# Seven products for both column halves of an FFN's last block pair, with weight sums made by adding transfers

## The chip, the cores and the metric

The kernel runs on one core of one Trainium2 chip, in one launch. The metric is the device time of that core in microseconds (us). Three timed runs before the change gave 2164.31, 2165.05 and 2165.15 us, median 2165.05. The profile was taken from a further execution, which took 2164.99 us; its span, from the first to the last instruction, is 2163.2 us, so 1.8 us lie around it.

## The reference

Two layers work on 256 tokens of width 2048 in float32. Each layer has a mixer stage and then a dense SwiGLU FFN of hidden width 5632. Only the FFN matters here:

```python
h = rms_norm(x, g[2])
f = (jax.nn.silu(h @ ffn_w_gate[layer]) * (h @ ffn_w_up[layer])) @ ffn_w_down[layer]
x = x + rms_norm(f, g[3])
```

## The kernel before

**Three matmuls for one product.** A float32 weight tile of 128x1024 (512 KB) is split into a high part `whi`, a rounded copy (ScalarE, L198), and a low part `wlo`, the rest (VectorE, L200). Activations are split the same way. TensorE then computes high x high, high x low and low x high (L237 to L239, or L771 to L773 in the products below) into one PSUM bank. `halves` makes both parts; each pool of parts has 7 tiles. A weight chunk of 512x512 is two such tiles, and with 256 tokens and three matmuls for one product it costs 24 matmuls of 512 columns.

**Two streams of weights.** `wstream` is loaded by `load_half` (tile `raw`, 5 buffers) in the order of use. `sstream` holds the down-projection chunks for the block pairs and is loaded by `sload` (tiles `sw`), as two tiles for one chunk. Both are issued on SyncE's queue.

**The FFN.** The 5632 hidden columns are 11 blocks of 512: five pairs (`PAIRS`) and one lone block (`LONE` = 10). For each block `gate_up` computes gate, up and their product, transposed. For a pair of blocks, the token halves t = 0, 1, the blocks and two neighbouring output columns n0, n1 form a 2x2 by 2x2 block matrix product. `quads` computes it with seven products of 12 matmuls each, where the plain way has eight. `combos` makes the seven operand combinations of the activations (tiles `so`), and `form` makes the weight sums in place with VectorE additions of 128x1024 (L720), two for each sum (one for each tile of a chunk). The products are called b11, t1, t2, b22, t3, b21, t4. Each goes into a PSUM bank `sq` and is added from there to one or two accumulators `f`, or to a helper accumulator `fu` that is folded in at the end (L780; the fold is L644 and L646). The 2048 output columns are four pieces of 512, n = 0 to 3; a column half p holds pieces 2p and 2p+1.

**What runs beside what.** `quads` is a generator. The matmul loops call `tick`, which moves it on by `rate` steps for each unit of work; one step is one half product of 6 matmuls. The products of a pair so run spread over the `gate_up` of the next pair. Only those of the last pair run beside the lone block.

**The last pair before.** By `COLS`, the pair (8, 9) runs `quads` for p = 1 only, at rate .75 beside the lone block's gate and up, and what is left beside its down products. The left columns, n = 0 and 1, are computed plainly for blocks 8, 9 and 10 in `post` (three chunks of 24 matmuls for each n), where `operand` chooses b11, a21, b21, t4 or the lone block's `ht`. For n = 2 and 3 only block 10 is left. `before(2)` lets all products finish before n = 2 begins.

**After the last product.** `post` adds each `acc` bank to `f` (L508, VectorE), takes its sum of squares (L398, ScalarE), and multiplies by the gain `gb` (L561). For n = 0 (both t) and for n = 1 (t = 0) that multiplication runs on GpSimd; the others are on VectorE. GpSimd's instructions and the transfers that it issues (`gb` at L492, the reload of `x` at L790) stand in one queue.

Each engine takes its instructions in the order that the scheduler fixed when the kernel was built, and waits at the first one that isn't ready.

Of the kernel before, what the change touches and what calls it, by code (L numbers as in the profile page):

```python
# [18 lines left out]
F32 = mybir.dt.float32  # L19
# [16 lines left out]
PAIRS = [(0, 1), (2, 3), (4, 5), (6, 7), (8, 9)]  # L36
COLS = [(0, 1)] * 4 + [(1,)]
LONE = 10
# [6 lines left out]
RATE1, WIDTH1 = .9, 7  # L45
NCHUNK = 306
NQUAD = 72
LHALF = (9, 10, 331, 332)
AHEAD, SETTLE = 2, 4
ENDRATE = .75  # L50
LAG = 2
# [43 lines left out]
class Trunk:  # L95
    def __init__(self, tc, dr, out, stage=99):
        self.tc, self.nc, self.dr, self.out, self.stage = tc, tc.nc, dr, out, stage
        self.plan = []
        self.pending = deque()
        self.bg = []  # L100
        self.early = deque()
        self.script, self.later = None, deque()
        self.lag = 2 * LAG
        self.nraw = 0
        self.rate, self.width, self.credit = 1.0, 3, 0.0
        self.n = 0
# [4 lines left out]
        self.splan, self.sraw, self.squeue = [], {}, deque()  # L111

# [475 lines left out]
    def ffn(self, li, norm, after):  # L588
# [20 lines left out]
        self.rate, self.width = 1.0, 1  # L609
        for pi, pair in enumerate(PAIRS):  # L610
            self.squeue.extend((li, b, n) for p in COLS[pi] for b, n in (
                (pair[0], 2 * p), (pair[0], 2 * p + 1), (pair[1], 2 * p + 1), (pair[1], 2 * p)))
        for pi, pair in enumerate(PAIRS):
# [12 lines left out]
            while self.bg:  # L626
                self.step()
            ops = self.combos(h, pi == len(PAIRS) - 1)
            self.spawn(self.quads(li, pair, COLS[pi], ops, f, pi == 0))
        ht = self.new_xt(1, "ht")  # L630
# [4 lines left out]
        def before(n):  # L635

            if n == 2:
                while self.bg:
                    self.step()
                self.tight = False  # L640
# [7 lines left out]
        def operand(kt, t):  # L648
            b, k = kt // 4, kt % 4
            if b == 2:  # L650
                return self.xk(ht)(k, t)
            o = ops[(("b11", "a21"), ("b21", "t4"))[b][t]]
            return o[0][:, k], o[1][:, k]
        self.rate = ENDRATE
        gate_up(LONE, whole)
        seg = self.post(li, 3, 1, after, f[:2], before)
        own = [(b, 4 * i) for i, b in enumerate((*PAIRS[-1], LONE))]
        seg(lambda n: [("ffn_w_down", li, 512 * b, 512 * n, k) for b, k in (own[2:] if n > 1 else own)], operand)

    def sload(self):  # L660

        if not self.squeue:
            return
        li, b, n = self.squeue.popleft()
        with self.tc.high_priority():
            tiles = [self.slot([P, 1024], nm="sw") for _ in range(2)]
            for i, r in enumerate(tiles):
                self.tc.keep_in_program_order(self.nc.sync.dma_start(
                    out=r, in_=self.dr["sstream"][len(self.splan)][:, i * 1024:(i + 1) * 1024]))
        self.splan.append(("A", "ffn_w_down", li, 512 * b, 512 * n))  # L670
        self.sraw[li, b, n] = tiles

    def combos(self, h, whole):


        nc = self.nc
        out = {}

        def put(key, src):
            o = self.slot([P, 2, 4, P], F32R, "so")  # L680
            out[key] = o[:, 0], o[:, 1]
            part(key, src)

        def part(key, src):
            hi, lo = out[key]
            nc.scalar.copy(hi, src)
            nc.vector.tensor_sub(lo, src, hi.bitcast(F32))
        put("b11", h[0, 0])
# [13 lines left out]
        put("t3", k)  # L702
        if whole:
            out["a21"] = self.mtmp([P, 4, P], F32R, "a21"), self.mtmp([P, 4, P], F32R, "a21")
            part("a21", h[1, 0])
        return out

    def quads(self, li, pair, cols, ops, f, first):

        nc = self.nc  # L710
        for _ in range(SETTLE):
            yield
        for p in cols:
            n0, n1 = 2 * p, 2 * p + 1
# [47 lines left out]
            for key in order:  # L762
# [13 lines left out]
                for d, sign, new in into[key]:  # L776
                    if first and new:
                        nc.scalar.copy(d, ps)
                    else:
                        (nc.vector.tensor_add if sign > 0 else nc.vector.tensor_sub)(d, d, ps)  # L780
                yield

# [834 lines left out]
```

## Time and profile before

| what | value |
|---|---|
| median of three runs | 2165.05 us |
| profiled execution | 2164.99 us, span 2163.2 us |
| TensorE busy | 2146.1 us, 99% |
| VectorE busy | 1741.8 us, 81% |
| ScalarE busy | 1244.1 us, 58% |
| GpSimd busy | 133.8 us, 6% |
| moved by DMA | 428.72 MB |

In profile rows PE is TensorE, PEld its weight loads, DVE VectorE, ACT ScalarE, POOL GpSimd and SP SyncE; a q behind the name is that engine's sequencer. A row of a group of instructions gives line, engine, operation, output tile, input tile, shape and count, then the busy time in us and the mean duration of one in ns, then the idle time ahead of them and what ended it. A row of the timeline gives the start in us, the duration in us, and the instruction; neighbours of one kind are merged, with their count. A matmul of 512 columns is recorded with 0.39 us but the next one starts after about 0.23 us, since matmuls are pipelined.

### The profile page before, as it was taken

To read this page: it belongs to the slowest core of one execution; us is meant where nothing else is said; L and a number is where in the kernel's file an instruction comes from. 1 tells how busy PE (TensorE), PEld (TensorE's weight loads), DVE (VectorE), ACT (ScalarE), POOL (GpSimd) and SP (SyncE) were. 2 spreads that over 40 slices of the span, in tenths; PEclk is the share of its full clock that TensorE was granted. 3 is DMA by queue.
4 is the path that set the end of the run, shared out by engine and by line. 5 is a ranking of instruction groups with operands and counts; after the bars stand their busy time and mean duration, and the time that the engine had idled before them with its cause. 6 is when DMAs were issued, how large, how long until landed. Compare 5 with 4: busy or idle time off the path is not lost.

```text
span 2163.2 us, 28371 instructions
## 1 busy us (share of the span) xinstructions
PE 2146.1 (99%) x10412; PEld 1788.6 (83%) x10412; DVE 1741.8 (81%) x2227; ACT 1244.1 (58%) x1692; POOL 133.8 (6%) x188
## 2 busy tenths in 40 slices
PE   9999999999999999999999999999999999999998
PEld 7888888888888888888878978888888888888886
DVE  6897765767878898898879997675788889889886
ACT  7655545565555555555557676565555555555553
POOL 0000110110000000000011231020000000000001
PEclk9999999999999999999999999999999999999999
DMA  8445566674565556567467654667456655556654
GB/s 294 150 148 162 185 202 192 203 275 149 196 237 194 198 180 206 172 205 244 159 220 238 208 181 142 222 211 271 160 197 204 214 203 187 190 186 203 218 174 147
DMA packets 118827, 428.72 MB, mean 198 GB/s; under 512 B 13584, under 2 KB 13744, under 8 KB 118688
## 3 DMA queue, kind: packets, MB, share of 16 engines
q1 hardware_dynamic: 110448, 399.65, 55.2%
q0 software_dynamic: 7664, 26.21, 3.6%
q8 instruction: 81, 1.33, 0.3%
q10 hardware_dynamic: 576, 1.05, 0.1%
q14 instruction: 58, 0.48, 0.1%
HBM read 418.44 MB, written 8.42 MB: 197 GB/s over the span
## 4 chain that ended last, share of the span: by engine, by line
PE 77%; issue 2%; DVE 1%; POOL 0%; ACT 0%; DVEq 0%; POOLq 0%; ACTq 0%
PE acc L239 18%; PE acc L237 18%; PE acc L238 18%; PE sq L772 5%; PE sq L773 5%; PE sq L771 5%; PE accb L337 1%; PE accb L338 1%; PE accb L339 1%; PE tp L380 1%; PE yp L1423 0%; DVE x L532 0%; PE apo L1166 0%; DVE wlo L200 0%; PE as L1112 0%
## 5 line engine op out<-in xcount | busy, mean ns | idle before, releaser
L200 DVE TENSOR_TENSOR wlo<-raw,whi 128x1024 fp32r<-128x1024 f32 x606 | 742.1, 1233 | 282.1 <-ACT whi L198 271.8
L198 ACT CAST whi<-raw 128x1024 fp32r<-128x1024 f32 x606 | 637.5, 1054 | 520.4 <-PE acc L239 264.4
L239 PE MATMUL acc<-whi,xt 128*128 128x512 f32 x1728 | 673.8, 391 | 1.0 <-DVE xt L409 1.0
L238 PE MATMUL acc<-wlo,xt 128*128 128x512 f32 x1728 | 673.5, 391 | 0.1
L237 PE MATMUL acc<-whi,xt 128*128 128x512 f32 x1728 | 673.4, 392 | 0.0
L198 ACT CAST whi<-sw 128x1024 fp32r<-128x1024 f32 x252 | 266.0, 1056 | 226.3 <-PE acc L239 124.8
L239 PEld LDWEIGHTS acc<-whi,xt 128*128 128x128 f32 x1728 | 324.4, 188 | 69.6 <-DVE xt L409 2.8
L237 PEld LDWEIGHTS acc<-whi,xt 128*128 128x128 f32 x1728 | 324.3, 188 | 67.6 <-issue 1.5
L238 PEld LDWEIGHTS acc<-wlo,xt 128*128 128x128 f32 x1728 | 324.5, 188 | 67.3 <-DVE wlo L200 0.6
L200 DVE TENSOR_TENSOR wlo<-sw,whi 128x1024 fp32r<-128x1024 f32 x252 | 306.9, 1221 | 40.5 <-ACT whi L198 36.4
L773 PE MATMUL sq<-whi,so 128*128 128x512 f32 x504 | 196.2, 389 | 0.0
L772 PE MATMUL sq<-wlo,so 128*128 128x512 f32 x504 | 196.2, 389 | 0.0
L771 PE MATMUL sq<-whi,so 128*128 128x512 f32 x504 | 196.0, 391 | 0.0
L720 DVE TENSOR_TENSOR sw<-sw,sw 128x1024 f32<-128x1024 f32 x144 | 174.8, 1220 | 6.2 <-DMA sw<-sstream 5.3
L773 PEld LDWEIGHTS sq<-whi,so 128*128 128x128 f32 x504 | 94.6, 188 | 19.8
L772 PEld LDWEIGHTS sq<-wlo,so 128*128 128x128 f32 x504 | 94.6, 188 | 19.4
L771 PEld LDWEIGHTS sq<-whi,so 128*128 128x128 f32 x504 | 94.6, 188 | 19.4
L238 PE MATMUL acc<-wlo,mixh 128*128 128x512 f32 x256 | 97.6, 391 | 0.0
L239 PE MATMUL acc<-whi,mixl 128*128 128x512 f32 x256 | 97.3, 390 | 0.0
L237 PE MATMUL acc<-whi,mixh 128*128 128x512 f32 x256 | 96.5, 393 | 0.0
L296 PE MATMUL acc<-xt,whi 128*128 128x512 f32 x384 | 95.8, 394 | 0.0
L780 DVE TENSOR_TENSOR f<-f,sq 128x512 f32<-128x512 f32 x128 | 84.9, 682 | 12.7 <-PE sq L773 12.6
(298 smaller groups left out, 2219.0 us busy)
## 6 DMA issues: line engine op xcount, KB each, us to landing
raw<-wstream SPq DMA_DIRECT2D x612, 512.0 KB, 4.7
sw<-sstream SPq DMA_DIRECT2D x144, 512.0 KB, 7.5
gb<-norm_gains POOLq DMA_DIRECT2D x16, 256.0 KB, 5.4
xm<-x POOLq DMA_DIRECT2D x16, 256.0 KB, 4.9
x<-xm POOLq DMA_DIRECT2D x8, 512.0 KB, 5.7
acb<-acrows POOLq DMA_DIRECT2D x8, 512.0 KB, 5.1
x<-x POOLq DMA_DIRECT2D x4, 512.0 KB, 7.4
xf<-x POOLq DMA_DIRECT2D x8, 256.0 KB, 4.8
```

The lines of the kernel that those rows point to most:

```text
L198: self.pin(nc.scalar.copy(hi, src))
L200: self.pin(nc.vector.tensor_sub(lo, src, hi.bitcast(F32)))
L237: self.pin(nc.tensor.matmul(ps[t], xh, wh[:, k % 2], start=s, stop=False))
L238: self.pin(nc.tensor.matmul(ps[t], xh, wl[:, k % 2], start=False, stop=False))
L239: self.pin(nc.tensor.matmul(ps[t], xl, wh[:, k % 2], start=False, stop=e))
L296: nc.tensor.matmul(ps, w[kt // 8][0][:, kt % 8], self.joined(kt, xt), start=kt == 0, stop=kt == 15)
L337: nc.tensor.matmul(ps, wh[:, kt % 8], xh, start=kt == 0, stop=False)
L720: nc.vector.tensor_add(a, a, b)
L771: nc.tensor.matmul(ps, xh, wh[:, k], start=s, stop=False)
L772: nc.tensor.matmul(ps, xh, wl[:, k], start=False, stop=False)
L773: nc.tensor.matmul(ps, xl, wh[:, k], start=False, stop=e)
L780: (nc.vector.tensor_add if sign > 0 else nc.vector.tensor_sub)(d, d, ps)
```

## The change

The last pair now takes seven products for both column halves. The plain chunks of blocks 8 and 9 are gone; `operand`, `a21` and `COLS` with them. The left half, p = 0, is formed as before by VectorE additions and runs beside the lone block's gate and up, at rate 1.1. The right half, p = 1, is "grown" (`GROWN`): its products run beside the lone block's down products of n = 0 and 1, at rate 5, and its weight sums are made by adding transfers that GpSimd issues (`grow`): each reads a further 512 KB from `sstream` and adds it to a tile that is already there. No VectorE addition forms them. The order of the grown products is b11, b22, t1, t3, t2, b21, t4: in one tile pair b11's weights become t1's, then t2's, then t4's; in another b22's become t3's. Right after `halves` has read a tile, `grow` is issued on it. `before(0)` now waits for the end of p = 0, and `before(2)` for the end of p = 1.

```diff
-COLS = [(0, 1)] * 4 + [(1,)]
+GROWN = [(PAIRS[-1], 1)]
...
-NCHUNK = 306
-NQUAD = 72
+NCHUNK = 298
+NQUAD = 80
...
-ENDRATE = .75
+ENDRATE = 1.1, 5
...
+            if n % 2 == 0:
+                self.until(lambda: self.done > n // 2)
+                self.rate = ENDRATE[1]
+                self.tight = n == 0
...
-        own = [(b, 4 * i) for i, b in enumerate((*PAIRS[-1], LONE))]
-        seg(lambda n: [("ffn_w_down", li, 512 * b, 512 * n, k) for b, k in (own[2:] if n > 1 else own)], operand)
+        seg(lambda n: [("ffn_w_down", li, 512 * LONE, 512 * n, 0)], self.xk(ht))
...
+    def grow(self, piece, key, i):
+
+        with self.tc.high_priority():
+            self.tc.keep_in_program_order(
+                self.nc.gpsimd.dma_start(out=piece, in_=self.spiece(key, i), accum_op=ALU.add))
...
+            grown = (pair, p) in GROWN
+            if grown:
+                order = ("b11", "b22", "t1", "t3", "t2", "b21", "t4")
...
+            home = {"b11": (0, n0), "b22": (1, n1), "t1": (0, n0), "t3": (1, n1), "t2": (0, n0), "b21": (1, n0), "t4": (0, n0)}
+            then = {"b11": (0, n1), "b22": (0, n1), "t1": (1, n1), "t2": (1, n0)}
...
-                    w = form(key)
+                    w = r(*home[key]) if grown else form(key)
                     for i in range(2):
                         ready.append(self.halves(w[i]))
+                        if grown:
+                            if key in then:
+                                b, n = then[key]
+                                self.grow(w[i], (li, pair[b], n), i)
+                            elif i:
+                                self.sload()
+                            yield
+                            continue
```

The built program shows where the scheduler put this. On GpSimd's queue, at the end of the second FFN, there stood before (`gb` the gain, `f` the accumulators, `x` the reloaded residual):

```order
L492 DMA gb_3727_18385<-norm_gains 128x512
L561 TENSOR_TENSOR f_2631_13172<-f_2631_13172,gb_3724_18379 128x512
L561 TENSOR_TENSOR f_2633_13174<-f_2633_13174,gb_3724_18379 128x512
L561 TENSOR_TENSOR f_2631_13172<-f_2631_13172,gb_3725_18381 128x512
L790 DMA x_3782_18674<-xm10_9859 128x1024
```

And now, at the same place (`sw_3717` and `sw_3718` are the two tiles that hold b11, t1, t2 and t4 in turn, `sw_3733` and `sw_3734` those of b22 and t3):

```order
L675 DMA sw_3717_18291<-sstream 128x1024
L675 DMA sw_3718_18292<-sstream 128x1024
L675 DMA sw_3733_18374<-sstream 128x1024
L675 DMA sw_3734_18375<-sstream 128x1024
L675 DMA sw_3717_18291<-sstream 128x1024
L675 DMA sw_3718_18292<-sstream 128x1024
L561 TENSOR_TENSOR f_2646_13201<-f_2646_13201,gb_3754_18477 128x512
L675 DMA sw_3717_18291<-sstream 128x1024
L561 TENSOR_TENSOR f_2648_13203<-f_2648_13203,gb_3754_18477 128x512
L675 DMA sw_3718_18292<-sstream 128x1024
L561 TENSOR_TENSOR f_2646_13201<-f_2646_13201,gb_3755_18479 128x512
L801 DMA x_3811_18731<-xm10_9888 128x1024
```

The eight adding transfers came in ahead of the reload of `x`; the last two, which make t4's weights, each stand behind a multiplication for n = 0, the first behind that of t = 0, the second behind that of t = 1.

On VectorE, where the lone block's down products of n = 0 are added to `f` (L508), there stood before:

```order
L200 TENSOR_TENSOR wlo_3771_18611<-raw_3753_18506,whi_3770_18609 128x1024
L200 TENSOR_TENSOR wlo_3774_18617<-raw_3761_18562,whi_3773_18615 128x1024
L508 TENSOR_TENSOR f_2631_13172<-f_2631_13172,acc_3734_18402 128x512
L508 TENSOR_TENSOR f_2633_13174<-f_2633_13174,acc_3738_18420 128x512
L200 TENSOR_TENSOR wlo_3777_18647<-raw_3764_18568,whi_3776_18645 128x1024
```

And now (`sq_3780` is the bank of t1, `sw_3743` and `sw_3744` hold b21's weights):

```order
L200 TENSOR_TENSOR wlo_3791_18630<-sw_3718_18292,whi_3790_18628 128x1024
L200 TENSOR_TENSOR wlo_3794_18644<-sw_3743_18412,whi_3793_18642 128x1024
L508 TENSOR_TENSOR f_2646_13201<-f_2646_13201,acc_3764_18500 128x512
L789 TENSOR_TENSOR f_2647_13202<-f_2647_13202,sq_3780_18573 128x512
L789 TENSOR_TENSOR f_2649_13204<-f_2649_13204,sq_3780_18573 128x512
L200 TENSOR_TENSOR wlo_3796_18654<-sw_3744_18413,whi_3795_18652 128x1024
L508 TENSOR_TENSOR f_2648_13203<-f_2648_13203,acc_3774_18542 128x512
```

The two additions that stood side by side are now separated by two additions of a product and one split, and they stand behind the split of t2's second tile (`wlo_3791`).

On TensorE, around the middle of the last product t4 (`sq_18714`), the order is now, with `acc_18749` the lone block's n = 1, t = 1:

```order
L782 MATMUL sq_18714<-whi_18683,so_17953 128x512
L780 MATMUL sq_18714<-whi_18693,so_17953 128x512
L237 MATMUL acc_18749<-whi_18741,hth_17976 128x512
L781 MATMUL sq_18714<-wlo_18695,so_17953 128x512
L782 MATMUL sq_18714<-whi_18693,so_17953 128x512
L780 MATMUL sq_18714<-whi_18693,so_17953 128x512
L781 MATMUL sq_18714<-wlo_18695,so_17953 128x512
L782 MATMUL sq_18714<-whi_18693,so_17953 128x512
L238 MATMUL acc_18749<-wlo_18743,hth_17976 128x512
```

All that is left behind t4 are the lone block's matmuls. Between the last matmul of n = 0 (t = 1) and the first that reads t4's second low part (`wlo_18695`) TensorE now has 50 matmuls of 512 columns: 6 of t3, 12 of t2, 12 of b21, 12 of the lone block's n = 1 (t = 0), 7 of t4 and 1 of `acc_18749`.

More of the change, by code (lines that the diff above doesn't have):

```diff
@@ L609, in ffn @@
         self.rate, self.width = 1.0, 1
-        for pi, pair in enumerate(PAIRS):
-            self.squeue.extend((li, b, n) for p in COLS[pi] for b, n in (
-                (pair[0], 2 * p), (pair[0], 2 * p + 1), (pair[1], 2 * p + 1), (pair[1], 2 * p)))
+        for pair in PAIRS:
+            for p in range(2):
+                own = [(li, pair[i], 2 * p + j) for i, j in ((0, 0), (0, 1), (1, 1), (1, 0))]
+                self.squeue.extend(own if (pair, p) not in GROWN else (own[0], *own[2:]))
+                for key in own:
+                    self.sidx[key] = len(self.splan)
+                    self.splan.append(("A", "ffn_w_down", li, 512 * key[1], 512 * key[2]))
         for pi, pair in enumerate(PAIRS):
@@ L627, in ffn @@
                 self.step()
-            ops = self.combos(h, pi == len(PAIRS) - 1)
-            self.spawn(self.quads(li, pair, COLS[pi], ops, f, pi == 0))
+            ops = self.combos(h)
+            self.done = 0
+            self.spawn(self.quads(li, pair, ops, f, pi == 0))
         ht = self.new_xt(1, "ht")
@@ L635, in before @@
         def before(n):
[L637 to L640, printed above, removed]
             if n % 2 == 0:
+                self.until(lambda: self.done > n // 2)
+                self.rate = ENDRATE[1]
+                self.tight = n == 0
                 u = f[2][:, n // 2 * 512:n // 2 * 512 + 512]
@@ L646, in before @@
                     nc.vector.tensor_sub(d, d, u)
[L648 to L654, printed above, removed]
+        self.rate = ENDRATE[0]
         gate_up(LONE, whole)
         seg = self.post(li, 3, 1, after, f[:2], before)
-        own = [(b, 4 * i) for i, b in enumerate((*PAIRS[-1], LONE))]
-        seg(lambda n: [("ffn_w_down", li, 512 * b, 512 * n, k) for b, k in (own[2:] if n > 1 else own)], operand)
+        seg(lambda n: [("ffn_w_down", li, 512 * LONE, 512 * n, 0)], self.xk(ht))
     def sload(self):
@@ L663, in sload @@
             return
-        li, b, n = self.squeue.popleft()
+        key = self.squeue.popleft()
         with self.tc.high_priority():
@@ L667, in sload, with spiece, combos @@
             for i, r in enumerate(tiles):
[L668 to L673, printed above, removed]
+                self.tc.keep_in_program_order(self.nc.sync.dma_start(out=r, in_=self.spiece(key, i)))
+        self.sraw[key] = tiles
+    def spiece(self, key, i):
+        return self.dr["sstream"][self.sidx[key]][:, i * 1024:(i + 1) * 1024]
+    def grow(self, piece, key, i):
+        with self.tc.high_priority():
+            self.tc.keep_in_program_order(
+                self.nc.gpsimd.dma_start(out=piece, in_=self.spiece(key, i), accum_op=ALU.add))
+    def combos(self, h):
         nc = self.nc
@@ L681, in put @@
             out[key] = o[:, 0], o[:, 1]
[L682 to L687, printed above, removed]
+            self.parts(src, *out[key])
         put("b11", h[0, 0])
@@ L702, in combos, with quads @@
         put("t3", k)
-        if whole:
-            out["a21"] = self.mtmp([P, 4, P], F32R, "a21"), self.mtmp([P, 4, P], F32R, "a21")
-            part("a21", h[1, 0])
         return out
-    def quads(self, li, pair, cols, ops, f, first):
+    def quads(self, li, pair, ops, f, first):
         nc = self.nc
@@ L712, in quads @@
             yield
-        for p in cols:
+        for p in range(2):
             n0, n1 = 2 * p, 2 * p + 1
@@ L780, in quads @@
                         (nc.vector.tensor_add if sign > 0 else nc.vector.tensor_sub)(d, d, ps)
+                if key == order[-1]:
+                    self.done = p + 1
                 yield
```

4 lines of the change are left out of this document (2 added, 2 removed).

## The prediction

> **What bounds the kernel now.** I read the page's busy shares first, then the chain that ended last, then the table by stage over the lone block of the second FFN.
>
> ```profile
> PE 2146.1 (99%) x10412; PEld 1788.6 (83%) x10412; DVE 1741.8 (81%) x2227; ACT 1244.1 (58%) x1692; POOL 133.8 (6%) x188
> PE 77%; issue 2%; DVE 1%; POOL 0%; ACT 0%; DVEq 0%; POOLq 0%; ACTq 0%
> 2070.00:2140.00 70.00, 70.00 (x313) 57.83 (x312) 52.74 (x54) 35.18 (x39) 3.95 (x2) 1.00 0.45 150
> ```
>
> The chain runs through TensorE, and in the 70 us of the lone block (columns: stretch, length, busy PE, PEld, DVE, ACT, POOL, granted clock, DMA share, GB/s) TensorE has no gap, at a granted clock of 1.00. So a matmul less is time less, but only if nothing makes TensorE wait in its place. VectorE has 70 - 52.74 = 17.3 us to spare there. The price of a matmul comes from two rows of the timeline with 22 steps between them, all of 512 columns:
>
> ```profile
> 2094.89 0.39 PE L237 MATMUL acc<-whi,xt 128*128 128x512 f32 x1
> 2099.88 0.39 PE L238 MATMUL acc<-wlo,xt 128*128 128x512 f32 x1
> ```
>
> 4.99 / 22 = 0.2268 us.
>
> **What is removed.** For the left columns of the last pair the plain way takes four chunks of 24 matmuls, 96; seven products of 12 are 84. That is 12 matmuls less for each FFN, 24 in all: 24 x 0.2268 = **-5.44 us**. This is all that can be won.
>
> **What VectorE and ScalarE get.** Four chunks cost eight splits; the new products cost 14, so six splits more for each FFN, and ten more additions from PSUM. The eight VectorE weight additions (L720) move from p = 1 to p = 0 and keep their number. `a21`'s split goes (0.69, by the split of `so`).
>
> ```profile
> L198 ACT CAST whi<-sw 128x1024 fp32r<-128x1024 f32 x252 | 266.0, 1056 | 226.3 <-PE acc L239 124.8
> L200 DVE TENSOR_TENSOR wlo<-sw,whi 128x1024 fp32r<-128x1024 f32 x252 | 306.9, 1221 | 40.5 <-ACT whi L198 36.4
> L720 DVE TENSOR_TENSOR sw<-sw,sw 128x1024 f32<-128x1024 f32 x144 | 174.8, 1220 | 6.2 <-DMA sw<-sstream 5.3
> L780 DVE TENSOR_TENSOR f<-f,sq 128x512 f32<-128x512 f32 x128 | 84.9, 682 | 12.7 <-PE sq L773 12.6
> L687 DVE TENSOR_TENSOR so<-hT,so 128x512 fp32r<-128x512 f32 x30 | 20.5, 685 | 0.0
> ```
>
> VectorE: 6 x 1.221 + 10 x 0.682 - 0.685 = 13.5 us for each FFN, into 17.3 us of spare time, while TensorE's work there gets 2.7 us shorter: 1.1 us of cover is left. ScalarE gets 6 x 1.056 us into 34.8 spare. I cost both at nothing as work, but VectorE is now so full that what stands behind another instruction there is late. If the cover were gone wholly, its price would be the few us by which the sum is exceeded.
>
> **What is moved: the weight sums of p = 1.** b11's tiles become t1's, t2's and t4's by three adding transfers each, one after the other, each waiting for the split before it, and with each split waiting for the transfer before it. The trace holds no adding transfer. The nearest rows are the plain transfers of 512 KB that GpSimd issues: the four reloads of `x` at the end of this FFN, 0.54 us apart, and the slowest group of four.
>
> ```profile
> L790 POOL DMA_DIRECT2D x<-xm x4: 537/537/577, 2142.6 to 2144.2; - x4
> DMA to landing us min/median/max: 4.3/5.6/6.8
> ...
> L790 POOL DMA_DIRECT2D x<-xf x4: 530/530/627, 1373.5 to 1375.2; - x4
> DMA to landing us min/median/max: 5.9/7.5/11.8
> ...
> DMA to landing us min/median/max: 3.6/4.1/5.3
> ```
>
> The first of the first four took 4.3 us from issue to landing, the last 6.8; so one transfer more in the queue costs (6.8 - 4.3 + 3 x 0.54) / 3 = 1.37 us. An adding transfer has to read its destination besides its source; as an estimate I count that as one more transfer of 512 KB. The last row is that of the `raw` loads around the lone block: the median lies 0.5 us above the minimum, which I take for the company of that stream. L = 4.3 + 1.37 + 0.5 = **6.2 us**, bounds 4.3 (an adding transfer as quick as a plain one) and 11.8. A gain is excluded: the additions that it replaces weren't waited for by TensorE.
>
> The Trainium skill speaks to this in "Collectives: The Full Stack", section "The bandwidth ceiling: the fold count and why AG ≠ RS ≠ AR": a reduction in a DMA engine has two source reads on one ring and so goes half as fast as a copy. No run here shows it so far. By that rule the data share of 1.37 us doubles, 5.7 us without company, against 4.3 if it weren't so; the difference is 2 x 1.4 = 2.8 us of kernel time by the sum below.
>
> **Where the transfers are waited for.**
>
> ```profile
> 2106.54 0.60 PE L380 MATMUL tp<-ca,h 128*128 128x128 f32 x4
> ```
>
> For t1 and t2 there is room. From the end of the lone block's up product TensorE has 60 matmuls and two groups of four transposes until t1's second half, some 14.7 us, and 30 matmuls (6.8 us) more until t2's second half; b11's second split is done at about the start of that time. t1's second half is ready after L + 1.06 + 1.22 = 8.5 us, t2's after 17, against 14.7 and 21.5. t4 is the tight one, since on GpSimd's queue its two transfers stand behind the multiplications for n = 0. How late those are, before shows directly, n = 0 having ended with the first row:
>
> ```profile
> 2122.91 0.39 PE L239 MATMUL acc<-whi,htl 128*128 128x512 f32 x1
> 2122.84 1.28 DVE L508 TENSOR_TENSOR f<-f,acc 128x512 f32<-128x512 f32 x2
> 2124.29 0.63 ACT L398 ACTIVATE sq<-f 128x512 bf16<-128x512 f32 x1
> 2125.85 0.62 ACT L398 ACTIVATE sq<-f 128x512 bf16<-128x512 f32 x1
> 2125.09 3.95 POOL L561 TENSOR_TENSOR f<-f,gb 128x512 f32<-128x512 f32 x2 [60.02 <-ACT sq L398]
> ```
>
> From the last matmul's start to the end of the second multiplication: 2125.09 + 3.95 - 2122.91 = 6.13 us. In the new order two additions and a split (2 x 0.68 + 1.22 = 2.6 us) stand between the two L508; some 0.9 us of that is hidden, since the second multiplication could have begun at 2126.5 but GpSimd was busy until 2127.4 (the first took 2.29):
>
> ```profile
> L561 POOL TENSOR_TENSOR f<-f,gb x3: 1289/1712/2285, 2125.1 to 2141.3; 128x512 f32<-128x512 f32 x3
> ```
>
> So t4's second low part is ready 6.13 + 1.7 + 6.2 + 1.06 + 1.22 = 16.3 us after that matmul's start. TensorE gets there 51 steps after it, 51 x 0.2268 = 11.6 us. **It waits 4.7 us**, once for each FFN; in general L - 1.5 us.
>
> Two small ones. The transposes of the lone block's last product now come right behind its matmuls and wait for `h` (0.74 us), which stands behind a split: 0 to 0.8 us, I take 0.4.
>
> ```profile
> 2100.42 0.74 DVE L602 SCALAR_TENSOR_TENSOR h<-acc,nrs,sg 128x512 f32<-128x512 f32 x1
> ```
>
> Behind t4 the lone block's next split follows t4's last on VectorE: 1.22 us against five matmuls, 1.13 us, and a handover: I take 0.3, bounds 0 and 0.6. The tail after the last matmul stays, since nothing of the change stands there; the reload of `x` stands behind the third multiplication, as before.
>
> **The sum.** For each FFN -2.72 + 4.7 + 0.4 + 0.3 = +2.7 us, for two +5.4. Against the profiled execution's 2164.99 us (span 2163.2 and 1.8 around it; 0.06 below the median): **2170.4 us**.
>
> **The rivals.**
> - *The sums land as plain transfers do, and t4 is hardly waited for.* L = 4.3 and the late L508 hidden: the wait is 4.3 - 3.2 = 1.1 us for each FFN, the sum -5.44 + 2.2 = -3.2, 2161.8; with the late L508 it is 2.8 us and 2165 to 2166. For it: the transfers stand 3 us apart, so each has the queue for itself, and the DMA share in the lone block is 0.45. Against it: the destination must be read.
> - *All of the gain is kept (not slower, but faster).* One mechanism: the multiplications for n = 0 leave GpSimd early enough that t4's transfers are issued 6.2 + 2.3 us ahead of need, that is within 3.1 us of the last matmul of n = 0. It decides below that point, and gives 2159.6 to 2160.7. Against it: addition 0.68, squares 0.63 and multiplication 1.3 to 2.3 alone come to 2.6 to 3.6 us before any waiting, and before measured 6.13.
> - *The transfers are slow, and the whole chain stands on them.* With L = 11.8, t1 is ready at 14.1 (just in time), t2 at 28.2 against 21.5, 6.7 us late, and t4 14.1 us after that against 38 matmuls, 8.6 us: 5.5 more. 12.2 + 0.7 - 2.72 for each FFN is +20.4 in all, 2185.4; still slower adding would cost more. For it: six of them are in flight one behind the other on one queue. Against it: no plain one near here takes over 6.8.
> - That the change wouldn't do what it says is excluded by the built order: both halves stand there as seven products, with the transfers in place.
>
> **How the numbers follow.** The forecast (L from 5.6 to 8, about 2168 to 2176) gets 0.45, the plain speed (2161 to 2168) 0.25, the slow chain (2176 and above) 0.18, the kept gain 0.12. The range leaves out a tenth at each end: 2160.5, just within the kept gain, to 2190, above the slow chain's price for its six transfers in one queue. A measurement of this kernel can tell about 0.2% from no change, 2160.7 to 2169.4. Faster is the kept gain, 0.12; the same is the plain speed and the forecast's lower part (0.08), 0.33; slower is the rest of the forecast and the slow chain, 0.55.
>
> **What would show it.** The matmul count falls by 24, 12 for each FFN. TensorE's idle time ahead of the matmuls of `sq` appears at t4, twice, some 4 to 5 us, released by VectorE's or ScalarE's split, which waited for the transfer; ahead of t1 and t2 nearly none. The adding transfers' rows show 5.6 to 8 us from issue to landing. The forecast is wrong if these rows show 4.3 or less, or if they show over 10, or if GpSimd's multiplications for n = 0 end well before 6 us after the last matmul of n = 0.

## The result, and the profile after

The changed kernel takes **2185.33 us** (median of 5 runs, 2183.53 to 2186.04); the kernel before, beside it, 2165.15 us (5 runs, 2164.31 to 2165.72). The ratio is 1.009, with a 95% interval of 1.0079 to 1.0102: slower. The direction and the range of the prediction held (2160.5 to 2190.0), the forecast of 2170.4 us lies 15 us too low. The profiled execution took 2185.81 us, its span is 2183.7 us, 20.5 more than before.

The page's first part, of the changed kernel (busy us, share of the span, number of instructions):

```profile
PE 2153.1 (99%) x10388; PEld 1788.4 (82%) x10388; DVE 1764.2 (81%) x2257; ACT 1252.3 (57%) x1702; POOL 150.5 (7%) x204
```

24 matmuls fewer than before, as announced, and TensorE is still busy 7 us longer (2146.1 before): a busy TensorE can also be one that runs slower. The view of what TensorE waited for, over the whole span (engine, line, whom it waited for; us in all, times, longest):

```profile
PE sq L780 <- ACT whi L198: 7.0, 2, 4.4
PE acc L238 <- DVE wlo L200: 2.3, 6, 0.6
...
PE tp L380 <- DVE x L532: 2.1, 2, 1.8
PE sq L781 <- DVE wlo L200: 2.1, 2, 1.1
PE acc L237 <- ACT whi L198: 1.6, 3, 1.3
```

The products (`sq`) and the lone block's chunks between them (`acc`) wait for splits, which before they never did. The two long waits for `whi`, 4.4 us in the first FFN and 2.6 in the second, stand ahead of the second half of t4. The GpSimd line that issues the adding transfers (duration of the issue min/median/max, and the time from issue to landing):

```profile
L675 POOL DMA_DIRECT2D sw<-sstream x16: 853/862/915, 1082.0 to 2147.3; - x16
...
DMA to landing us min/median/max: 5.4/7.9/10.1
```

The median is 7.9 us where the prediction took 6.2. How they follow one another is seen on ScalarE, whose cast starts when a tile has landed (timeline of ScalarE, second FFN), and in the windows view (the column before the last is the DMA share, the last GB/s):

```profile
2129.82 1.05 ACT L198 CAST whi<-sw 128x1024 fp32r<-128x1024 f32 x1 [4.24 <-DMA sw<-sstream]
2132.31 1.05 ACT L198 CAST whi<-sw 128x1024 fp32r<-128x1024 f32 x1 [1.43 <-DMA sw<-sstream]
2134.80 1.05 ACT L198 CAST whi<-sw 128x1024 fp32r<-128x1024 f32 x1 [1.44 <-DMA sw<-sstream]
...
2148.82 1.05 ACT L198 CAST whi<-sw 128x1024 fp32r<-128x1024 f32 x1 [2.91 <-DMA sw<-sstream]
2154.32 1.04 ACT L198 CAST whi<-sw 128x1024 fp32r<-128x1024 f32 x1 [4.45 <-DMA sw<-sstream]
```

```profile
2120.00:2130.00 10.00, 10.00 (x47) 8.28 (x46) 6.94 (x9) 3.57 (x5) 3.39 (x4) 1.00 1.04 190
```

The casts are 2.49 us apart, and the DMA engines are full at only 190 GB/s: 512 KB in 2.49 us is 210 GB/s. t3's two transfers and t2's two stand in the queue one behind the other (issued 2119.97 to 2127.13, below; the first three casts above and one at 2137.26 follow on them), and each takes 9.8 to 10.1 us. t4's two, issued with those gone, reach their casts (the last two rows) after 5.5 and 7.0 us. What that does to t4 stands in two timelines of the second FFN, of GpSimd and of VectorE:

```profile
2119.97 0.86 POOL L675 DMA_DIRECT2D sw<-sstream  x1 [1.85 <-DVE wlo L200]
2122.36 0.86 POOL L675 DMA_DIRECT2D sw<-sstream  x1 [1.53 <-DVE wlo L200]
2124.64 0.86 POOL L675 DMA_DIRECT2D sw<-sstream  x1 [1.43 <-DMA sw<-sstream]
2127.13 0.85 POOL L675 DMA_DIRECT2D sw<-sstream  x1 [1.63 <-DVE wlo L200]
2142.14 1.27 POOL L561 TENSOR_TENSOR f<-f,gb 128x512 f32<-128x512 f32 x1 [14.16 <-ACT sq L398]
2143.36 0.87 POOL L675 DMA_DIRECT2D sw<-sstream  x1
2146.00 1.37 POOL L561 TENSOR_TENSOR f<-f,gb 128x512 f32<-128x512 f32 x1 [1.77 <-ACT sq L398]
2147.32 0.87 POOL L675 DMA_DIRECT2D sw<-sstream  x1
```

```profile
2138.34 2.36 DVE L200 TENSOR_TENSOR wlo<-sw,whi 128x1024 fp32r<-128x1024 f32 x2 [1.23 <-ACT whi L198]
2140.62 0.68 DVE L508 TENSOR_TENSOR f<-f,acc 128x512 f32<-128x512 f32 x1
2141.22 1.28 DVE L789 TENSOR_TENSOR f<-f,sq 128x512 f32<-128x512 f32 x2
2142.41 2.08 DVE L200 TENSOR_TENSOR wlo<-sw,whi 128x1024 fp32r<-128x1024 f32 x1
2144.41 0.68 DVE L508 TENSOR_TENSOR f<-f,acc 128x512 f32<-128x512 f32 x1
...
2155.39 1.23 DVE L200 TENSOR_TENSOR wlo<-sw,whi 128x1024 fp32r<-128x1024 f32 x1 [2.21 <-ACT whi L198]
```

t4's two transfers are issued at 2143.36 and 2147.32, each right behind a multiplication, as predicted. But the multiplications are later than predicted: the first L508 stands on VectorE behind two splits (the second tile of t2, the first of b21), and that of t2 had waited for its adding transfer. The last matmul of n = 0 starts at 2136.15, so the second multiplication ends 2147.37 - 2136.15 = 11.2 us after it, where the prediction had 6.13 + 1.7 = 7.8.

Then comes what was not foreseen. The timeline of TensorE behind the wait, and the windows view there (the column ahead of the DMA share is the granted clock):

```profile
2152.47 0.39 PE L782 MATMUL sq<-whi,so 128*128 128x512 f32 x1
2155.41 0.79 PE L780 MATMUL sq<-whi,so 128*128 128x512 f32 x1 [2.56 <-ACT whi L198]
...
2156.95 0.63 PE L781 MATMUL sq<-wlo,so 128*128 128x512 f32 x1
...
2161.65 0.59 PE L238 MATMUL acc<-wlo,hth 128*128 128x512 f32 x1
2162.07 0.40 PE L239 MATMUL acc<-whi,htl 128*128 128x512 f32 x1
```

```profile
2155.00:2160.00 5.00, 4.43 (x10) 3.22 (x11) 4.61 (x5) 4.77 (x7) 0.14 (x1) 0.52 0.00 0
```

From 2156.95 to 2161.65 eleven steps of one matmul take 0.427 us each instead of 0.227, at a granted clock of 0.52: the clock fell to half at the end of the wait, and stayed there for some 6.8 us. From 2155.41 to 2162.07 lie 14 steps; 6.66 - 14 x 0.2268 = 3.5 us are lost in the second FFN, 0.15 of it a wait. In the first FFN the same stretch, 11 steps from 1122.52 to 1127.87, loses 2.9 us.

**Where the 20.5 us are.** Two markers split the span: the last `accl` matmul (right behind the first FFN) and the last matmul of `mixh` (end of the second layer's mixer). Their start in the tile views, in us; in brackets the difference from before:

| | last `accl` | last `mixh` | span | first FFN / mixer / second FFN |
|---|---|---|---|---|
| before | 1163.4 | 1445.6 | 2163.2 | |
| after | 1172.7 (+9.3) | 1457.3 (+11.7) | 2183.7 (+20.5) | +9.3 / +2.4 / +8.8 |

What TensorE loses is best counted from its starts: every step from one matmul to the next beyond 0.2268 us. (The waits view understates a gap, since it counts from a matmul's modelled end, 0.39 us behind its start.) In the second FFN these losses are 8.7 us up to t4's second half, 8.0 of them from 2136.15 to 2155.41 (4.3 at t4's two halves, 3.7 ahead of t4, most of it at the lone block's chunks), and 3.5 us of half clock behind it: 12.2 - 2.7 for 12 matmuls = 9.5, against the 8.8 measured. In the first FFN they are 13.6 us, 2.9 of them half clock; before, the wait for the second layer's `x` alone was some 2. 13.6 - 2 - 2.7 = 8.9, against 9.3. The middle 2.4 us lie in a place where the change edits nothing; the experiments come back to it.

### The profile page after: what moved, and what is told of

It reads as the page before. It is cut to its first block, busy times and chain, and to the rows that moved or that the text cites. A ratio compares the mean times of both kernels' runs of the same rounds, so it can differ in the third digit from the quotient of the medians.

```text
span 2183.7 us, 28389 instructions
## 1 busy us (share of the span) xinstructions
PE 2153.1 (99%) x10388; PEld 1788.4 (82%) x10388; DVE 1764.2 (81%) x2257; ACT 1252.3 (57%) x1702; POOL 150.5 (7%) x204
## 4 chain that ended last, share of the span: by engine, by line
PE 70%; issue 6%; DMA 1%; DVE 1%; POOL 1%; ACT 0%; DVEq 0%; POOLq 0%; ACTq 0%
PE acc L237 17%; PE acc L239 17%; PE acc L238 17%; PE sq L782 5%; PE sq L781 5%; PE sq L780 5%; DMA sw<-sstream 1%; PE accb L337 1%; PE accb L338 1%; PE accb L339 1%; PE tp L380 1%; PE yp L1434 0%; DVE wlo L200 0%; PE apo L1177 0%; DVE x L532 0%
## 5 line engine op out<-in xcount | busy, mean ns | idle before, releaser
L200 DVE TENSOR_TENSOR wlo<-raw,whi 128x1024 fp32r<-128x1024 f32 x590 | 721.9, 1233 | 263.3 <-ACT whi L198 253.1
L198 ACT CAST whi<-raw 128x1024 fp32r<-128x1024 f32 x590 | 619.1, 1053 | 514.4 <-PE acc L239 317.9
L198 ACT CAST whi<-sw 128x1024 fp32r<-128x1024 f32 x280 | 294.9, 1055 | 260.7 <-PE acc L239 142.1
L200 DVE TENSOR_TENSOR wlo<-sw,whi 128x1024 fp32r<-128x1024 f32 x280 | 341.7, 1226 | 67.0 <-ACT whi L198 63.4
L780 PE MATMUL sq<-whi,so 128*128 128x512 f32 x560 | 219.1, 394 | 7.0 <-ACT whi L198 7.0
L781 PE MATMUL sq<-wlo,so 128*128 128x512 f32 x560 | 219.6, 392 | 2.3 <-DVE wlo L200 2.1
L782 PE MATMUL sq<-whi,so 128*128 128x512 f32 x560 | 219.2, 391 | 0.0
L780 PEld LDWEIGHTS sq<-whi,so 128*128 128x128 f32 x560 | 105.7, 189 | 30.0 <-ACT whi L198 8.7
L781 PEld LDWEIGHTS sq<-wlo,so 128*128 128x128 f32 x560 | 105.7, 189 | 25.6 <-DVE wlo L200 4.2
L782 PEld LDWEIGHTS sq<-whi,so 128*128 128x128 f32 x560 | 105.7, 189 | 21.8
L789 DVE TENSOR_TENSOR f<-f,sq 128x512 f32<-128x512 f32 x144 | 95.6, 682 | 7.3 <-PE sq L782 7.3
```

The source lines that it names most:

```text
L198: self.pin(nc.scalar.copy(hi, src))
L200: self.pin(nc.vector.tensor_sub(lo, src, hi.bitcast(F32)))
L780: nc.tensor.matmul(ps, xh, wh[:, k], start=s, stop=False)
L781: nc.tensor.matmul(ps, xh, wl[:, k], start=False, stop=False)
L782: nc.tensor.matmul(ps, xl, wh[:, k], start=False, stop=e)
```

## The experiments

All are the changed kernel with one or two edits, and each ratio is to the kernel before, run beside it on the same chip (its medians there 2165.52 to 2166.52 us, 2165.15 beside the changed kernel, so times of runs on different chips compare to about 1 us).

### Who makes the sums

The weight sums of p = 1 made by VectorE, with no adding transfer:

```diff
-GROWN = [(PAIRS[-1], 1)]
+GROWN = []
```

> Both halves of the last pair as seven products, but the weight sums of p = 1 made by VectorE's additions, with no adding transfer. Theory (the loss is the adding transfers and what stands on them): the 24 matmuls fewer stay, VectorE gets 8 x 1.22 = 9.8 us more for each FFN than in the changed kernel, 23.3 us against the 17.3 spare of before, so some 3 to 6 us late for each FFN at most: 2160 to 2172 us. Rival (the two sets of products beside the lone block are too dense by themselves, whoever makes the sums): 2180 us or more.

Measured: 2181.9 us, ratio 1.0075 (1.0062 to 1.0088). The theory's number fails, and the rival's is hit. The windows view of this run (the third busy column is VectorE):

```profile
2140.00:2150.00 10.00, 8.25 (x35) 6.06 (x34) 10.00 (x10) 5.32 (x6) 1.56 (x1) 1.00 0.11 34
2150.00:2160.00 10.00, 8.17 (x35) 5.89 (x34) 10.00 (x13) 1.78 (x3) 0.98 (x1) 1.00 0.06 20
```

VectorE has no gap from 2120 to 2160 us, and TensorE waits for it. So this version is slow for another reason than the changed kernel: VectorE's work, 23.3 us against 17.3 of room, where the expectation of "3 to 6 us" forgot that this work falls due in the last 40 us. That the products are not "too dense by themselves, whoever makes the sums", the rival's reason, is shown below, by the run without any sums.

The same sums on GpSimd:

```diff
 GROWN = []
-                        nc.vector.tensor_add(a, a, b)
+                        (nc.gpsimd if pair == PAIRS[-1] and p == 1 else nc.vector).tensor_add(a, a, b)
```

> Both halves as seven products, no adding transfers, the eight additions of 128x1024 for p = 1 of the last pair on GpSimd instead of VectorE (some 2.6 us each by the 1.3 us of its 128x512 multiplication, 21 us in the 67 us). Theory (VectorE's load is what made 2181.9 us of the version with VectorE's additions): 2162 to 2170 us. Rival (VectorE's splits get slower beside GpSimd, 2.1 instead of 1.2 us as in the changed kernel, and give the time back): 2172 to 2182 us.

Measured: 2190.27 us, ratio 1.0114 (1.01 to 1.0127), slower than either. The groups of GpSimd and of VectorE in the last 100 us:

```profile
L715 POOL TENSOR_TENSOR sw<-sw,sw 128x1024 f32<-128x1024 f32 x8 | 22.3, 2813 | 48.1 <-DVE wlo L200 48.1
```

```profile
L200 DVE TENSOR_TENSOR wlo<-sw,whi 128x1024 fp32r<-128x1024 f32 x21 | 35.7, 1718 | 1.3 <-ACT whi L198 1.1
L200 DVE TENSOR_TENSOR wlo<-raw,whi 128x1024 fp32r<-128x1024 f32 x14 | 16.9, 1218 | 2.5 <-ACT whi L198 2.3
```

A sum takes GpSimd 2.81 us, and the splits of `sw`, which fall beside these sums, take 1.72 us instead of 1.22: 21 x 0.5 = 10.5 us more of VectorE, more than the 9.8 that it was spared. The rival's reason shows, but its range (2172 to 2182) lies too low: the eight sums also take GpSimd 22.3 us, and ScalarE's casts wait 8.9 us for them.

### What the adding transfers cost

The same transfers in the same places, without adding:

```diff
-                self.nc.gpsimd.dma_start(out=piece, in_=self.spiece(key, i), accum_op=ALU.add))
+                self.nc.gpsimd.dma_start(out=piece, in_=self.spiece(key, i)))
```

> The same transfers on GpSimd's queue, in the same places, but overwriting instead of adding: the additions into the weight sums of p = 1 are left out. Theory (adding is what makes them slow): 4.3 to 5.5 us from issue to landing, about 1.4 us apart where they queue up instead of 2.49, t2's splits earlier and so VectorE less late; the wait at t4 falls to 1 to 3 us for each FFN: 2161 to 2172 us. Rival (an adding transfer costs what a plain one does, the place in the queue is the matter): within 4 us of the changed kernel, 2181 us or more.

Measured: 2172.05 us, ratio 1.0028 (1.0018 to 1.0037), 13.3 us below the changed kernel: the theory, at the upper end of its range. GpSimd's line in this run:

```profile
L675 POOL DMA_DIRECT2D sw<-sstream x16: 527/530/593, 1082.1 to 2135.3; - x16
...
DMA to landing us min/median/max: 3.9/5.2/6.0
```

To issue one takes 0.53 us instead of 0.86, to land 5.2 instead of 7.9. Of the single edits that keep the transfers, this one gains most.

No transfers at all, and nothing in their place:

```diff
     def grow(self, piece, key, i):
+        return
```

> The changed kernel without its adding transfers and with nothing in their place: the additions into the weight sums of p = 1 of the last pair are left out, all products, splits and their order stay. Theory A (VectorE's 13.5 us more are hidden in its spare time, all of the loss is waiting for transfers): 24 matmuls less show, 2159.5 to 2163 us, TensorE waits under 1 us around the products. Theory B (VectorE is too full in the last 40 us of an FFN, transfers or not): 2165 to 2171 us, with TensorE waiting for splits and VectorE without a gap there.

Measured: 2166.83 us, ratio 1.0005 (0.9996 to 1.0014). Theory B's number, but not its mechanism: in the second FFN TensorE waits 0.3 us in all, and from the last `mixh` (1450.7, +5.1) to the end (2165.5, +2.3) the full 2.8 us are won. The gain is lost ahead of that: +1.9 at the last `accl`, +3.2 in the mixer. Some 0.9 of the 1.9 us is there before the change begins: the last `mixh` matmul of the first layer starts at 423.5 us, 422.5 before. The first FFN still costs 1 us more than before, where 2.7 less was to be won, and its end shows how. The kernel before, timelines of TensorE and of VectorE:

```profile
1128.13 0.63 PE L380 MATMUL tp<-ca,x 128*128 128x128 f32 x4 [1.87 <-issue]
```

```profile
1127.28 1.42 DVE L532 SCALAR_TENSOR_TENSOR x<-f,prs,x 128x512 f32<-128x512 f32 x2 [0.29 <-POOL prs L556]
```

The run without transfers, timelines of TensorE and of VectorE, and its windows view:

```profile
1128.14 1.12 PE L380 MATMUL tp<-ca,x 128*128 128x128 f32 x4 [3.85 <-DVE x L532]
...
1136.03 0.60 PE L380 MATMUL tp<-ca,x 128*128 128x128 f32 x4
```

```profile
1127.33 1.42 DVE L532 SCALAR_TENSOR_TENSOR x<-f,prs,x 128x512 f32<-128x512 f32 x2 [2.15 <-DMA x<-xm]
```

```profile
1130.00:1135.00 5.00, 5.00 (x17) 4.00 (x16) 4.32 (x6) 2.68 (x8) 1.08 (x2) 0.58 0.84 281
```

The second layer's first transposes start at the same time in both, 1128.13 and 1128.14: they need the norm's `x` (L532). Before, that waited for the norm's factor `prs`; here it waits for the reload of `x`, which lands at 1127.24, where before the first part landed at 1125.22 (6.9 us from issue to landing against 4.3). TensorE's 2 us turn into 2 us more of waiting, and behind this wait of 3.85 us the clock falls (0.58): the third transposes follow the first after 7.89 us, 5.06 before (1128.13 to 1133.19). So the fewer matmuls of the first FFN cost time there. The reload is not the only thing that holds this place: with both edits of a run below (transfers without adding, multiplications on VectorE) it lands some 20 us earlier, `x` waits for `prs` again, and the transposes start no sooner, at 1128.81.

### The clock

Sixteen matmuls of 512 columns more for each FFN, around t4's halves, on ready operands, their result unread:

```diff
+                    if grown and key == "t4":
+                        spare = self.mx([P, 512], "wm") if i == 0 else spare
+                        for _ in range((4, 12)[i]):
+                            nc.tensor.matmul(spare, xh, wh[:, 1], start=True, stop=True)
                     next(ahead, None)
```

> The changed kernel with 16 matmuls of 512 columns more for each FFN, around t4's two halves, on operands that are ready, into a PSUM tile that nobody reads. Theory (the granted clock falls because TensorE idles there, and that costs 3.2 us for each FFN): of the 3.6 us of added matmuls some 3 lie in the waits, the clock stays at 1.00 behind them: 2178 to 2182 us. Rival (the clock falls for another reason): the time rises by the part not hidden, 2186 to 2193 us, with the clock still at about a half behind t4.

Measured: 2185.68 us, ratio 1.0092 (1.0078 to 1.0106), no change; neither range is hit. In the second FFN the clock holds:

```profile
2155.00:2160.00 5.00, 4.46 (x18) 3.22 (x18) 5.00 (x5) 3.73 (x6) 1.88 (x2) 1.00 0.00 0
```

From the last `mixh` to the end this run takes 1.5 us less than the changed kernel (724.9 against 726.4): of the 3.5 us of half clock, part is paid, it seems, for matmuls that did not fit into the wait. In the first FFN, whose wait is longer, the clock fell all the same (0.73 from 1120 to 1125 us), for 3.4 us instead of 6.8. So the median shows nothing, and the trace shows for one place of two that filling the wait holds the clock.

The clearer test takes the run without transfers (weight sums left out as there) and fills the wait at the layer's border:

```diff
+                        if c == "T0" and given and li == 0:
+                            spare = self.mx([P, 4, P], "wm")
+                            for k in range(40):
+                                self.pin(nc.tensor.matmul(spare[:, k % 4, :], self.ident, self.ident, start=True, stop=True))
```

> The version without adding transfers (weight sums of p = 1 left out), with 40 matmuls of 128x128 on the identity ahead of the first transposes of the second layer's x, where TensorE waited 3.85 us and then ran at half clock (128 columns cost 0.09 us each by the transposes, 3.6 us). Theory (the clock falls because TensorE idled for close to 4 us, and that half clock cost 2.8 us: third transposes 7.9 us behind the first instead of 5.1): the granted clock stays at 1.00 there, the third transposes follow the first after 5.1 us, 2 to 3 us less: 2164 to 2165.5 us. Rival (the clock's fall has another cause, or small matmuls don't hold it): the clock still falls, 2166.5 us or more.

Measured: 2168.03 us, ratio 1.0012 (1.0003 to 1.0021); the expected time is missed, because the 40 matmuls took 9.1 us instead of 3.6:

```profile
1123.98 9.10 PE L529 MATMUL wm<-ca 128*128 128x128 f32 x80
1132.91 0.60 PE L380 MATMUL tp<-ca,x 128*128 128x128 f32 x4
...
1137.90 0.60 PE L380 MATMUL tp<-ca,x 128*128 128x128 f32 x4
```

The mechanism is as expected: the third transposes follow the first after 4.99 us again, at a clock of 1.00. The filler held the transposes back by some 4.8 us (1132.91 against 1128.14 without it), and the run lost only 1.2 us; the 2.8 us of half clock that it won back make up most of the difference.

### The place behind the multiplications

The norm's multiplications of the FFN all on VectorE:

```diff
-                        i = (nc.gpsimd if n < 2 - t else nc.vector).tensor_mul(out=p, in0=d, in1=gb[n])
+                        i = (nc.gpsimd if n < 2 - t and before is None else nc.vector).tensor_mul(out=p, in0=d, in1=gb[n])
```

> The FFN's norm multiplications for n = 0 and 1 go to VectorE, so that nothing stands ahead of t4's two adding transfers on GpSimd's queue. Theory (the place behind the multiplications is most of the loss): t4's second transfer is issued at the end of t2's second split, some 6 us earlier, the waits at t4 go and the clock stays at 1.00; VectorE pays about 1.5 us for each FFN: 2163 to 2169 us. Rival (the transfers' own 6 to 8 us and their 2.49 us pace are most of it): still 4 us or more of waiting at t4 and the clock's fall behind it, 2176 to 2184 us.

Measured: 2178.15 us, ratio 1.0056 (1.0043 to 1.007), 7.2 us below the changed kernel: the rival's range, though its clock was wrong. In the second FFN the clock stays at 1.00 and the waits view sums to 3.3 us instead of 6.3, but VectorE has no gap from 2140 to 2160 us. In the first FFN the wait moved to the border (4.7 us for `x`, clock 0.70 behind it). So the place costs something, but less than the adding does.

t4's sum alone on VectorE, from tiles that are there anyway:

```diff
-            then = {"b11": (0, n1), "b22": (0, n1), "t1": (1, n1), "t2": (1, n0)}
+            then = {"b11": (0, n1), "b22": (0, n1), "t1": (1, n1)}
+                    if grown and key == "t4":
+                        add(r(0, n0), r(1, n0))
```

> t4's sum is made by two VectorE additions from b21's tiles instead of by two adding transfers; the other six stay. Theory (t4's two transfers behind GpSimd's multiplications, and the clock's fall behind them, are most of the loss): VectorE pays 2 x 1.22 = 2.4 us for each FFN, the waits at t4 go, 2167 to 2174 us. Rival (the six earlier transfers make VectorE's splits late, and that alone does most of it): the clock stays at 1.00, but TensorE waits for VectorE instead, 2176 to 2182 us.

Measured: 2181.57 us, ratio 1.0075 (1.0062 to 1.0087): the rival. t4's transfers are gone and 3.8 us with them. VectorE is full from 2140 to 2160 us, and TensorE waits 4.1 us for splits in the second FFN by the waits view; in the first it waits 5.7 us for `x`, with a clock of 0.50 behind it. Six additions moved from VectorE to GpSimd on top of that:

```diff
-                nc.vector.tensor_add(left[1], left[1], u)
+                nc.gpsimd.tensor_add(left[1], left[1], u)
                 for d in right:
-                    nc.vector.tensor_sub(d, d, u)
+                    nc.gpsimd.tensor_sub(d, d, u)
```

> As the run with t4's sum on VectorE, and the six additions of 128x512 with u (L648, L650 of the changed kernel) go from VectorE to GpSimd, 6 x 0.68 = 4.1 us off VectorE for each FFN. If VectorE is the bound behind the late transfers: 4 to 8 us below the run with t4's sum on VectorE. If the transfers are: within 2 us of it, or above it, since GpSimd takes 1.3 to 2.3 us for such an operation and the next product's sums wait for it.

Measured: 2179.13 us, ratio 1.0065 (1.0052 to 1.0077), 2.4 us less, between the two expectations: inconclusive, as the two intervals overlap.

Both single edits together, transfers without adding and multiplications on VectorE (the two diffs above):

> Transfers that overwrite instead of adding (the additions into p = 1's weight sums are left out) and the norm's multiplications for n = 0 and 1 on VectorE: both single edits together. If the place in GpSimd's queue costs something of its own, as the 7 us with adding transfers: 2163 to 2167 us. If it costs only because each adding transfer is long: 2169 to 2174 us, no better than the plain transfers alone (2172.05).

Measured: 2169.05 us, ratio 1.0016 (1.0007 to 1.0025). The place is worth 7.2 us with adding transfers (2185.33 to 2178.15) and 3.0 without (2172.05 to 2169.05). The time lies at the lower edge of the second expectation: a good half of what the place costs comes from the length of the transfers that stand there, not all of it.

### An earlier start

With the multiplications on VectorE, the products spread faster over the lone block:

```diff
-ENDRATE = 1.1, 5
+ENDRATE = 1.5, 5
```

> The version with the norm's multiplications on VectorE and adding transfers, its products spread faster over the lone block's gate and up products (rate 1.5 instead of 1.1), so that p = 1's chain of splits and adding transfers begins some 8 us earlier against the lone block. Theory (the chain's length from its start to need is what is short): the waits at the products go, 2166 to 2172 us. Rival (VectorE is full in any case): the waits move to the front, 2175 to 2182 us.

Measured: 2171.74 us, ratio 1.0029 (1.0017 to 1.0041): the theory. The first adding transfer is issued at 2096.53 instead of 2116.18 us. Half of these 20 us is this run's lead at the end of the mixer (last `mixh` 1447.5 against 1457.3), so within the FFN the chain starts some 10 us earlier, near the 8 expected. No product waits any more; in their place the lone block's last operand, with no products left to lie beside it, and behind this wait the clock is at half for 6.8 us:

```profile
PE acc L237 <- ACT hth L363: 3.2, 1, 3.2
```

That one number alone, the multiplications back on GpSimd:

> The changed kernel with one number changed: the rate at which its products are spread over the lone block's gate and up products is 1.5 instead of 1.1; the multiplications stay on GpSimd. Theory (what the change lacks is the time between the chain's start and its need): the first adding transfer is issued some 20 us earlier against the end as in the version with both edits (2096.5 instead of 2116.2), t4's two are issued before n = 0's multiplications, no wait at t4, and VectorE is spared 1.4 us for each FFN: 2168 to 2173 us. Rival (it needs the multiplications off GpSimd as well): 2176 us or more, with t4's transfers behind L561.

Measured: 2173.41 us, ratio 1.0033 (1.0022 to 1.0044), 11.9 us below the changed kernel, just above the theory's range. GpSimd's timeline shows its mechanism: t4's transfers now stand ahead of the multiplications. The earlier start is again 10 us within the FFN (2099.60, last `mixh` 1450.6), not the 20 of the expectation. At the border to the second layer this run waits 6.6 us for `x`, with half clock for 10.2 us.

```profile
2122.47 0.89 POOL L675 DMA_DIRECT2D sw<-sstream  x1 [4.70 <-DVE wlo L200]
2126.18 0.87 POOL L675 DMA_DIRECT2D sw<-sstream  x1 [2.82 <-DVE wlo L200]
2143.85 1.62 POOL L561 TENSOR_TENSOR f<-f,gb 128x512 f32<-128x512 f32 x1 [16.80 <-ACT sq L398]
```

The same two markers for the runs that carry the argument (differences from before; first FFN / mixer / second FFN):

| | last `accl` | last `mixh` | span | parts |
|---|---|---|---|---|
| transfers without adding | 1166.0 | 1450.7 | 2169.1 | +2.6 / +2.5 / +0.8 |
| no transfers | 1165.3 | 1450.7 | 2165.5 | +1.9 / +3.2 / -2.8 |
| rate 1.5, multiplications on VectorE | 1165.3 | 1447.5 | 2168.1 | +1.9 / 0.0 / +3.0 |
| rate 1.5 alone | 1168.4 | 1450.6 | 2171.5 | +5.0 / 0.0 / +3.3 |

The first part counts from the span's start: the run without transfers is already 0.9 us late, and that with rate 1.5 and multiplications on VectorE 0.9 us early, at the end of the first layer's mixer, ahead of the change. The other two are within 0.2 us of before.

The mixer's 2.4 to 3.2 us are there at rate 1.1 and gone at rate 1.5, though no line of it is edited. The groups of TensorE between 1165 and 1620 us, of before, of after and of the run with rate 1.5 alone:

```profile
L1423 PE MATMUL yp<-seg,xs 128*64 128x256 f32 x64 | 8.7, 392 | 0.0
```

```profile
L1434 PE MATMUL yp<-seg,xs 128*64 128x256 f32 x64 | 10.6, 394 | 0.0
```

```profile
L1434 PE MATMUL yp<-seg,xs 128*64 128x256 f32 x64 | 8.7, 392 | 0.0
```

In the program of the changed kernel the 64 short matmuls of `yp` stand in 11 stretches, broken by others, where before and at rate 1.5 they stand in 8 whole ones; their busy time goes from 8.7 to 10.6 us, 1.9 of the 2.4 us. In the run without transfers, whose mixer takes 3.2 us more, they stand in 12. In all runs of the two tables the time goes with this order; the order was not edited alone, so that it is the cause is argued, not shown.

## Why the prediction came out as it did

**Right.** The sign; the count of matmuls; that TensorE waits at t4, twice, 4.3 us in all in the second FFN, for a split that waits for a transfer behind GpSimd's multiplications; that t1 has room. The window was right too: from n = 0's last matmul to the start of t4's second half lie 49 steps, 11.1 us, and to its first low part the 51 predicted, 11.6. That VectorE's 13.5 us are hidden was right for the second FFN: without transfers TensorE waits 0.3 us there and 2.8 us are won.

**The size of L.** "L = 4.3 + 1.37 + 0.5 = 6.2 us" was sized for one transfer with the queue for itself. At t4, where it entered the sum, that nearly held: 5.5 and 7.0 us from issue to cast. Ahead of it, where "there is room", it did not: the median is 7.9, half of the sixteen took over 8, and t3's and t2's stood four in the queue at 2.49 us each and took some 10. The chain to t2 had left out t3's two transfers between. So the 4.5 us of room at t2 were used up, and its second half waits 0.3 us for its low part (at 2139.62). The Trainium skill, on the page "Collectives: The Full Stack", section "The bandwidth ceiling: the fold count and why AG ≠ RS ≠ AR", has the reducing step of a ring collective go half as fast as its copying step. The runs agree in kind: 2.49 against the 1.37 us by which the prediction's plain transfers followed one another is a factor of 1.8, and from issue to landing 7.9 against 5.2 us in the same places is 1.5.

**The term that failed most: "6.13 + 1.7".** The prediction carried the multiplications' lateness over from before and added what the change puts between them. But on VectorE they stand behind splits that themselves wait for adding transfers, so that L enters a second time: 11.2 us instead of 7.8. t4's second low part was ready at 2155.39 + 1.23, 20.5 us after that matmul, where the prediction had 16.3; 3.4 of these 4.2 us are the multiplication's lateness, 0.8 are L. Instead of 4.7 us TensorE so loses 8.9 up to there, part of it already ahead of t4, where other splits are late. That "in general L - 1.5 us" is too flat, since a longer L also makes the multiplications later, follows from this order; no run varied L alone in steps.

**What was missing.** Three costs stood nowhere in the sum. The clock falls behind the waits: 3.5 and 2.9 us here, and 2.8 us in the run without transfers. The first FFN's end is no free tail: there fewer matmuls only mean a longer wait for `x`, and behind it half clock, so that the half of the 5.44 us that lies there wasn't won even in the run without sums. And the order of a mixer that nobody edited changed, for 2.4 us.

**The rival with the right number.** The slow chain's 2185.4 us is the measured time, by accident: its price was 6.7 us at t2 and 5.5 at t4, and t2 waits 0.3 us. Its ground was half right all the same: transfers did stand one behind the other in the queue, four of them.

**The account.** From the 2159.7 us that 24 matmuls less would give: +7.1 with no sums at all (2166.83; border, clock and mixer, and the 0.9 us from ahead of the change), +5.2 for plain transfers in the places of the adding ones (2172.05), +13.3 for adding (2185.33). These steps hold in this order only: an earlier start with the adding kept wins 11.9 us too, some 2.4 of them in the mixer, so the costs are not separate sums. Since even sums for nothing only equal the kernel before, no version tried beats it; the fastest that computes all is 2171.74 us.

## What to carry to other kernels

Price a chain of transfers by the pace at which they follow one another and by every engine that one late link holds up, not by the time of a single one; and look for the instructions of other work that stand behind that link. Work taken off the busiest engine is won only where its next input comes earlier too: look at the border to the next stage before counting it. And give a chain an earlier start before making its links faster: one number did nearly as much here as taking the addition out of the transfers.

## What the hardware showed that was not expected

- TensorE's granted clock fell to half and came back on a grid of 3.41 us. At the FFNs' ends in the changed kernel it was at half from 1121.00 to 1127.83 and from 2155.24 to 2162.06 us, in other runs for 3.4 us (filler around t4, 1122.33 to 1125.74) or 10.2 us (rate 1.5 alone, 1127.05 to 1137.29). A matmul of 512 columns then took 0.427 us instead of 0.227.
- The length of one wait doesn't decide it. At the ends of the FFNs, over all runs, the clock fell only behind a stretch of this grid in which TensorE was busy 1.61 us or less, and never where it was busy 1.70 or more; from 1.55 to 1.61 both occur. So a stretch with a longest wait of 2.56 us was enough (2151.82 to 2155.24, busy 1.03), and so was one with 1.47 us and several smaller ones (six additions on GpSimd, 1110.79 to 1114.20, busy 1.61), while a wait of 3.54 us in that same run, which the grid cut in two (busy 1.57 and 1.70), was not. The Trainium skill, on the page "TensorE: Matmul & The Clock Gate", section "Part 1: The HAM clock gate (the "warmup" mystery)", states an idle window of about 3.4 us and, for one busy core, two states, half and full. The halves and the window's length agree; here the window needn't be idle throughout.
- A DMA that adds into SBUF moved 512 KB in 2.49 us (210 GB/s) with the DMA share at 1.04, and took GpSimd 0.86 us to issue instead of 0.53.
- VectorE's split of 128x1024 took 1.72 us beside GpSimd's additions and 1.22 without.
- Matmuls of 128x128 in full f32 on the identity counted twice (80 records for 40) and took 0.23 us each, where the transposes that were used to price them take 0.09.
